# Three of VectorE's tiles move from the input projection to the output projection, half a gate changes its place, and two sums change engine

## The chip, the cores and the metric

The kernel runs on one core of a Trainium2 chip. The metric is the device time of one execution in microseconds; less is better. The core has a matrix engine (TensorE, in the profile PE), a vector engine (VectorE, DVE), an activation engine (ScalarE, ACT), GpSimd (POOL) and a queue engine (SyncE, SP) that issues nearly all transfers from memory.

## The reference, cut to what matters

One residual block over 256 tokens of width 2048, in float32:

```
mod = silu(c) @ w_ada + b_ada;  sh1, sc1, gt1, sh2, sc2, gt2 = split(mod, 6)
h   = rms_norm(x, g_mix) * (1 + sc1) + sh1
qA, kA, vA, qB, kB, vB = split(h @ w_in)
oA  = windowed attention (16 heads);  oB = chunked attention (16 heads)
x   = x + gt1 * (concat[rms_norm(oA), rms_norm(oB)] @ w_out)
h   = rms_norm(x, g_ffn) * (1 + sc2) + sh2
x   = x + gt2 * moe(h)         # 32 experts, w_gate, w_up, w_down: 403 MB
shf, scf = split(silu(c) @ w_ada_final + b_ada_final)
y   = rms_norm(x, g_final) * (1 + scf) + shf
```

The vectors of `mod` are matrix-vector products: one row `silu(c)` with a wide matrix. All weights are read once.

## The kernel before, in words

All weights go through a ring of six slots of 2 MB (`Ring`, lines 45 to 81). Tiles are loaded strictly in the order in which they were added to the ring, by SyncE (line 72 for a plain tile), and a tile can be sent for when the tile six places ahead of it, and all before that, have been released; on the chip the transfer waits until the slot's last reader is done.

After a first stage (the first quarters, qA, kA and vA), 20 steps follow. Twelve of them are halves of the rest of the input projection W_in (`in_step`: qB0, kB0, vB0, qB1, kB1, vB1, two steps each). Eight are the output projection W_out (`out_step`, called wo0 to wo7 here): wo0 to wo3 multiply the attention's A half with four column blocks of W_out, wo4 to wo7 its B half. Each step has one tile for TensorE. In the ring, `VECTOR_TILES` says how many tiles for VectorE follow it.

VectorE's tiles are the matrix-vector products: tiles of 512 rows by 1024 columns, four for a half of a vector. `vec_steps` works the queue of them off, four instructions a tile (line 382 for the first of a half, 384 for the others), each adding 128 rows into an accumulator of 128 x 1024. There are two accumulators. A half that has all four tiles is summed over the partitions by TensorE and copied out by ScalarE (`vec_finish`, three calls of `weave` later), and only then its accumulator is free. The halves of the first gate, gt1, keep theirs until `spread_gt1` has spread them over the partitions: at the start of wo1 for the first half, of wo3 for the second. `vec_steps` stops where it would need a third:

```
while queue and most and not (queue[0][1] == 0 and queue[0][4] == 0 and len(accs) == 2):
    vec_step(*queue.pop(0))
```

Attention heads are woven into the steps. `weave(n)` first runs what is due in `later`, then starts `n` heads from `ready`, makes the values of those two calls back and the transposes of those one call back, and runs the new heads' scores in four stages, with `vec_steps(2)` behind each stage. If no heads are left, there are no stages and no tile steps. `in_step` calls `weave(0)` and `weave(2)`, `out_step` `weave(1)` and `weave(2)`; between the two the step's tiles are put in the queue and `vec_steps(4)` is called, and after the step `vec_steps()` without a bound. The heads run out in wo2.

In `scores`, VectorE takes the masked maximum of a head (485, 486) and the reciprocal of its denominator (503), ScalarE the exponentials, and GpSimd scales (504, 505). `bias_B` sends for the bias of the pair of heads after next on ScalarE's queue, and GpSimd sets a corner of it (464). In `values`, the square of each pair's output (ScalarE, 538) is added to a running sum (539); when a kind's last head is through, `norm_o` makes the norm factors `rO[kind]` of it (546, then lines 190 to 198 on VectorE; `r_oB` in the profile). `out_step` evacuates every product with that factor and the gate (VectorE, 622; two banks, tag `w`) and adds it to x (623: GpSimd for A, VectorE for B).

After wo7 come four tiles for `shf`, the routing, and the expert layer: eight groups of four experts, gate, up and down, 403 MB through the same ring (829, 857).

Of the kernel before, what the change touches and what calls it, by code (L numbers as in the profile page):

```python
# [19 lines left out]
ALU = mybir.AluOpType  # L20
# [3 lines left out]
D = 2048  # L24
# [11 lines left out]
NEG = -1e30  # L36
RING = 6

VECTOR_TILES = [2, 3, 2, 3, 2, 3, 2, 3, 2, 3, 2, 3, 2, 2, 2, 2, 3, 2, 1, 0]


ROW_ADA, ROW_FIN, ROW_MIX, ROW_FFN, ROW_GFIN, ROW_OA, ROW_OB = 0, 24, 32, 36, 40, 44, 46
# [42 lines left out]
def block_kernel(ctx: ExitStack, tc: tile.TileContext, a: dict):  # L85
    nc = tc.nc
    V, S, G, PE = nc.vector, nc.scalar, nc.gpsimd, nc.tensor
# [8 lines left out]
    ada, fin = a["w_ada"], a["w_ada_final"]  # L96
    w_in, w_out = a["w_in"], a["w_out"]

    def rows(w, row, n, col, width):

        return w[row : row + 128 * n, col : col + width].rearrange("(k p) n -> p k n", p=128)
# [6 lines left out]
        first_quarters.append((gemv, [ring.add((2, 1536), rows(w_in, q * 512 + h * 256, 2, 0, 1536)) for h in range(2)]))  # L108

    vec_tiles = []  # L110
    for name, w, col in (("sh2", ada, 3 * D), ("sc2", ada, 4 * D), ("gt2", ada, 5 * D), ("gt1", ada, 2 * D), ("scf", fin, D), ("shf", fin, 0)):
        for c in (0,) if name == "shf" else (0, 1024):
            vec_tiles += [((name, c // 512), k, 4, 1024, rows(w, k * 512, 4, col + c, 1024)) for k in range(4)]
    blocks = [("qB0", 1536), ("kB0", 2560), ("vB0", 3584), ("qB1", 2048), ("kB1", 3072), ("vB1", 4096)]
    pe_tiles = [(name, h, rows(w_in, h * 1024, 8, col, 512)) for name, col in blocks for h in range(2)]
    pe_tiles += [("wo", h * 4 + n, rows(w_out, h * 1024, 8, n * 512, 512)) for h in range(2) for n in range(4)]
    order = []
    for (name, h, src), count in zip(pe_tiles, VECTOR_TILES):
        part = ring.add((8, 512), src)
# [9 lines left out]
    for g in range(8):  # L129
# [11 lines left out]
        else:  # L141
# [4 lines left out]
            for n in range(2):  # L146
                c = 1024 + 512 * n
# [63 lines left out]
    with ExitStack() as sa:  # L211
# [4 lines left out]
        def bank(tag, name, bufs=2):  # L216
            return ps.tile([128, 512], F32, tag=tag, name=name, bufs=bufs)
# [84 lines left out]
        for q, (gemv, parts) in enumerate(first_quarters):  # L302
# [3 lines left out]
            for i, idx in enumerate(gemv):  # L306
                w = ring.get(idx)
                for k in range(4):
                    c = cact[:, 4 * i + k : 4 * i + k + 1]
# [28 lines left out]
            for c in range(4):  # L338
                k = 4 * q + c
# [4 lines left out]
            for c in range(4):  # L344
                kk = 4 * q + c
                w = ring.get(parts[c // 2])[:, c % 2, :]
# [170 lines left out]
        def values(kind, h):  # L517
            pt = live.pop(("T", kind, h))
            c = h // 2
            b = 64 * (h % 2)  # L520
            if h % 2 == 0:
                live["o"] = bank("v", f"op{kind}{c}", 1)
            op = live["o"]
            if kind == "A":
                v, col = vA, (h // 4) * 64
            else:
                v, col = half[f"vB{h // 8}"], (h % 8) * 64
            PE.matmul(op[b : b + 64, 0:256], lhsT=v[:, 0, col : col + 64], rhs=pt[:, 0:256], start=True, stop=False, skip_group_check=True)
            PE.matmul(op[b : b + 64, 128:256], lhsT=v[:, 1, col : col + 64], rhs=pt[:, 256:384], start=False, stop=True, skip_group_check=True)
            if h % 2:  # L530
                cc = c + (8 if kind == "B" else 0)
                S.activation(oT[:, cc, :], op[:, 0:256], AF.Identity, scale=goutc[:, cc : cc + 1])
                s = sq[kind]
                if c == 0:
                    S.activation(s, op[:, 0:256], AF.Square)
                else:
                    s2 = pa2.tile([128, SEQ], F32, tag="sq", name=f"sq{kind}{c}", bufs=1)
                    S.activation(s2, op[:, 0:256], AF.Square)
                    G.tensor_tensor(s, s, s2, op=ALU.add)
                if h == 15:  # L540
                    later.append([1, lambda: norm_o(kind)])

        def norm_o(kind):
            pm = bank("m", f"pn{kind}", 1)
            for t in range(2):
                PE.matmul(pm[:, t : t + 1], lhsT=sq[kind][:, t * 128 : (t + 1) * 128], rhs=ones[:, 0:1], start=True, stop=True)
            rO[kind] = rsqrt_mean(pm[:, 0:2], 1.0 / 1024, 2, f"o{kind}")
# [3 lines left out]
        def weave(n=1):  # L551

            for item in list(later):
                item[0] -= 1
                if item[0] <= 0:
                    later.remove(item)
                    item[1]()
            if not n:
                return
            batch, ready[:] = ready[:n], ready[n:]  # L560
            line.insert(0, batch)
            for depth, step in ((2, values), (1, turn)):
                if len(line) > depth:
                    for item in line[depth]:
                        step(*item)
            heads = [scores(*item) for item in batch]
            while heads:
                heads = [x for x in heads if next(x, "end") is None]
                vec_steps(2)
            del line[3:]  # L570
# [400 lines left out]
    for g in range(8):  # L971
# [56 lines left out]
        else:  # L1028
# [3 lines left out]
            for fc in range(4):  # L1032
                w = ring.get(dn[fc])
# [6 lines left out]
            for fc in range(2):  # L1040
                w = ring.get(dn[4 + fc])
# [4 lines left out]
            for n in range(2):  # L1046
                w = ring.get(dn[6 + n])
# [20 lines left out]
    for J, y in last.items():  # L1068
        c = slice(J * 512, (J + 1) * 512)
# [3 lines left out]
    for t, J, store in ((0, 0, 0), (0, 1, 2), (0, 2, 0), (0, 3, 2), (1, 0, 1)):  # L1073
        c = slice(J * 512, (J + 1) * 512)
        V.scalar_tensor_tensor(big[:, t, c], big[:, t, c], r3[:, t : t + 1], shbc[:, c], op0=ALU.mult, op1=ALU.add)
        if store:
            c = slice((J + 1 - store) * 512, (J + 1) * 512)
# [27 lines left out]
```

## Time and profile before

| | |
|---|---|
| median of 3 runs | 1508.41 us (1505.83 to 1509.24) |
| the profiled execution | 1502.64 us, its span 1501.0 us |
| TensorE (PE) | 1188.0 us busy, 79% of the span |
| VectorE (DVE) | 499.0 us, 33% |
| ScalarE (ACT) | 166.2 us, 11% |
| GpSimd (POOL) | 157.5 us, 10% |
| transfers | 599.38 MB, 399 GB/s on the mean |
| mean granted clock of TensorE | 0.917 |

The shares are averages over the span. The input projection with its attention heads lies between some 150 and 358 us, the output projection from there to 520 us, the routing around 530 us and the expert layer after 543 us. Times in the profile are microseconds from the span's start. A matmul of float32 stands as two instructions. A granted clock of 1.00 is TensorE's full clock. A DMA share of about 1.03 is what the busiest stretches show.

### The profile page before, as it was taken

What the parts mean: (1) busy time and instruction counts of PE and PEld (TensorE: products, weight loads), DVE (VectorE), ACT (ScalarE), POOL (GpSimd) and SP (SyncE); (2) the same over time, 40 slices, a digit from 0 to 9 for tenths busy, and PEclk for the clock granted to TensorE, in tenths of its full rate; (3) what the DMA queues carried; (4) which work ended last, traced back from release to release, by engine and by line L of the source; (5) the groups of instructions that cost most, each with busy time, mean ns of one, the idle gap of its engine ahead of it and who ended that gap; (6) DMA issues with size and microseconds to landing.
All of it is one profiled execution on the core that took longest, in us unless ns stands there. A gap on an engine that the chain in (4) does not pass through costs nothing.

```text
span 1501.0 us, 14175 instructions
## 1 busy us (share of the span) xinstructions
PE 1188.0 (79%) x5891; PEld 525.8 (35%) x5892; DVE 499.0 (33%) x807; ACT 166.2 (11%) x423; POOL 157.5 (10%) x144
## 2 busy tenths in 40 slices
PE   4889999999999997777677767766767667667786
PEld 2667865754444542222212212211211211221222
DVE  1453789887667531011111211111201201111113
ACT  2000222223220110000000100000000000000012
POOL 1000355523441100000000000000000000000002
PEclk9999999999999999978978889889889988997999
DMA  9999999999987999999999999999999999999995
GB/s 333 396 392 399 394 402 402 402 401 400 355 317 302 388 380 422 421 420 421 421 421 421 421 421 422 422 422 421 421 420 422 422 422 422 421 421 421 421 412 210
DMA packets 125470, 599.38 MB, mean 399 GB/s; under 512 B 5881, under 2 KB 8489, under 8 KB 78041
## 3 DMA queue, kind: packets, MB, share of 16 engines
q1 hardware_dynamic: 121248, 594.82, 98.1%
q10 hardware_dynamic: 4120, 3.57, 0.7%
q8 instruction: 48, 0.79, 0.2%
q14 instruction: 22, 0.17, 0.0%
q0 software_dynamic: 32, 0.02, 0.0%
HBM read 596.02 MB, written 2.12 MB: 398 GB/s over the span
## 4 chain that ended last, share of the span: by engine, by line
DMA 45%; PE 11%; SPq 0%; issue 0%; ACT 0%; DVE 0%; ACTq 0%; DVEq 0%
DMA ring<-w_down 23%; DMA ring<-w_up 12%; DMA ring<-w_gate 10%; PE yp L857 5%; PE gp L829 2%; PE up L829 2%; PE sc_g L876 0%; SPq L70 0%; PE bc L770 0%; PE bc L771 0%; PE last L1060 0%; PE last L1059 0%; ACT big L1071 0%; PE last L1070 0%; ACTq L1072 0%
## 5 line engine op out<-in xcount | busy, mean ns | idle before, releaser
L857 PE MATMUL yp<-ring,actT_g 128*32 128x512 f32 x1024 | 181.5, 763 | 97.5 <-DMA ring<-w_down 91.7
L829 PE MATMUL up<-ring,xg_g 128*32 128x512 f32 x1024 | 177.3, 721 | 73.3 <-DMA ring<-w_up 73.2
L829 PE MATMUL gp<-ring,xg_g 128*32 128x512 f32 x1024 | 169.9, 703 | 69.3 <-DMA ring<-w_gate 68.8
L878 DVE TENSOR_TENSOR x<-x,sc_g 128x512 f32<-128x512 f32 x64 | 44.0, 688 | 252.3 <-PE sc_g L876 252.3
L618 PE MATMUL po<-ring,oT 128*128 128x512 f32 x256 | 118.0, 617 | 1.4 <-DMA ring<-w_out 1.4
L857 PEld LDWEIGHTS yp<-ring,actT_g 128*32 128x32 f32 x1024 | 39.3, 133 | 225.6 <-DMA ring<-w_down 130.9
L881 POOL TENSOR_TENSOR big<-x,xg_gscf 128x512 f32<-128x512 f32 x8 | 10.0, 1272 | 958.8 <-DVE x L878 958.8
L799 DVE TENSOR_SCALAR xg_g<-g_g,gsc,sh2c 128x128 f32<-128x128 f32 x64 | 26.2, 410 | 249.8 <-PE g_g L790 232.5
L829 PEld LDWEIGHTS up<-ring,xg_g 128*32 128x32 f32 x1024 | 38.4, 127 | 197.5 <-DMA ring<-w_up 105.9
L829 PEld LDWEIGHTS gp<-ring,xg_g 128*32 128x32 f32 x1024 | 38.0, 123 | 186.5 <-DMA ring<-w_gate 99.5
L797 ACT ACTIVATE xg_g<-g_g,sh2c,gsc 128x128 f32<-128x128 f32 x64 | 29.3, 458 | 503.9 <-DVE xg_g L799 503.9
L384 DVE SCALAR_TENSOR_TENSOR acc_gt<-ring,cact,acc_gt 128x1024 f32<-128x1024 f32 x60 | 79.2, 1321 | 1.6
L870 DVE TENSOR_TENSOR ys_g<-yp,gt2bc 128x512 f32<-128x512 f32 x32 | 21.8, 690 | 171.8 <-PE yp L857 171.8
L618 PEld LDWEIGHTS po<-ring,oT 128*128 128x128 f32 x256 | 49.7, 198 | 63.6 <-issue 61.1
L790 PEld LDWEIGHTS g_g<-pn_g,big 128*128 128x128 f32 x512 | 60.5, 194 | 29.1 <-issue 28.2
L790 PE MATMUL g_g<-pn_g,big 128*128 128x128 f32 x512 | 66.7, 284 | 1.4 <-DVE pn_g L782 1.4
L348 PE MATMUL qA<-hT,ring 128*128 128x256 f32 x256 | 61.6, 396 | 4.8 <-DVE hT L343 3.5
L876 PE MATMUL sc_g<-ys_g,smat_g 128*128 128x512 f32 x128 | 63.4, 618 | 1.6 <-DVE ys_g L870 1.6
L585 PE MATMUL pw_vB<-ring,hT 128*128 128x512 f32 x128 | 56.7, 597 | 2.9 <-DMA ring<-w_in 2.9
L589 PE MATMUL pw_kB<-hT,ring 128*128 128x256 f32 x256 | 57.0, 381 | 1.2 <-DMA ring<-w_in 1.2
L589 PE MATMUL pw_qB<-hT,ring 128*128 128x256 f32 x256 | 56.5, 381 | 0.2 <-DMA ring<-w_in 0.2
L348 PEld LDWEIGHTS qA<-hT,ring 128*128 128x128 f32 x256 | 50.7, 199 | 13.1 <-DVE hT L343 4.3
(329 smaller groups left out, 1125.4 us busy)
## 6 DMA issues: line engine op xcount, KB each, us to landing
ring<-w_gate SPq DMA_DIRECT2D x64, 2048.0 KB, 20.3
ring<-w_up SPq DMA_DIRECT2D x64, 2048.0 KB
ring<-w_down SPq DMA_DIRECT2D x62, 2048.0 KB, 20.4
ring<-w_ada SPq DMA_DIRECT2D x32, 2048.0 KB, 17.0
ring<-w_ada SPq DMA_DIRECT2D x32, 1024.0 KB, 14.1
ring<-w_ada_final SPq DMA_DIRECT2D x16, 2048.0 KB, 11.0
ring<-w_in SPq DMA_DIRECT2D x12, 2048.0 KB, 16.8
ring<-w_out SPq DMA_DIRECT2D x8, 2048.0 KB
```

The lines of the kernel that those rows point to most:

```text
L348: PE.matmul(early[n // 2][:, (n % 2) * 256 : (n % 2 + 1) * 256], lhsT=w[:, n * 128 : (n + 1) * 128], rhs=hT[:, kk, :], start=kk == 0 and n ...
L384: V.scalar_tensor_tensor(accs[name], w[:, kk, :], cact[:, c : c + 1], accs[name], op0=ALU.mult, op1=ALU.add)
L585: PE.matmul(b[s], lhsT=hT[:, kk, s * 128 : (s + 1) * 128], rhs=w[:, k, :], start=kk == 0, stop=kk == 15)
L589: PE.matmul(b[s][:, n * 256 : (n + 1) * 256], lhsT=w[:, k, c * 128 : (c + 1) * 128], rhs=hT[:, kk, :], start=kk == 0 and n == 0, stop=kk = ...
L618: PE.matmul(b, lhsT=oT[:, (i // 4) * 8 + k, t * 128 : (t + 1) * 128], rhs=w[:, k, :], start=k == 0, stop=k == 7)
L790: PE.matmul(pm[:, i * 128 : (i + 1) * 128], lhsT=big[:, t, kk * 128 : (kk + 1) * 128], rhs=pn[:, t, :], start=t == 0 and i == 0, stop=t == ...
L797: S.activation(xg[:, kk, :], pm[:, i * 128 : (i + 1) * 128], AF.Identity, bias=sh2c[:, kk : kk + 1], scale=gsc2[:, kk : kk + 1])
L799: V.tensor_scalar(xg[:, kk, :], pm[:, i * 128 : (i + 1) * 128], gsc2[:, kk : kk + 1], sh2c[:, kk : kk + 1], op0=ALU.mult, op1=ALU.add)
L829: PE.matmul(bankt[32 * e : 32 * e + 32, :], lhsT=xg[:, kk, 32 * e : 32 * e + 32], rhs=w[e // 2][:, e % 2, j, :], start=kk == 0, stop=kk == ...
L857: PE.matmul(y[32 * e : 32 * e + 32, :], lhsT=aT[:, fc, 32 * e : 32 * e + 32], rhs=w(e)[:, n * 512 : (n + 1) * 512], start=fc == 0, stop=fc ...
L876: PE.matmul(pm, lhsT=sm[:, t * 128 : (t + 1) * 128], rhs=ys[:, n, :], start=True, stop=True)
L878: V.tensor_tensor(x1[:, t, c], x1[:, t, c], pm, op=ALU.add)
```

## The change

Three of the tiles that VectorE works on move from the steps of W_in (30 before, 27 now) to those of W_out (14 before, 17 now). Four tiles of the second gate, its second half, move behind the first gate, so that the order of the halves becomes sh2, sh2, sc2, sc2, gt2, gt1, gt1, gt2, scf, scf, shf. In `values`, the last addition of each kind's squares is made by VectorE and not by GpSimd.

```diff
-VECTOR_TILES = [2, 3, 2, 3, 2, 3, 2, 3, 2, 3, 2, 3, 2, 2, 2, 2, 3, 2, 1, 0]
+VECTOR_TILES = [2, 2, 3, 2, 2, 2, 3, 2, 2, 3, 2, 2, 3, 2, 3, 3, 3, 2, 1, 0]
...
     vec_tiles = []
-    for name, w, col in (("sh2", ada, 3 * D), ("sc2", ada, 4 * D), ("gt2", ada, 5 * D), ("gt1", ada, 2 * D), ("scf", fin, D), ("shf", fin, 0)):
-        for c in (0,) if name == "shf" else (0, 1024):
-            vec_tiles += [((name, c // 512), k, 4, 1024, rows(w, k * 512, 4, col + c, 1024)) for k in range(4)]
+    halves = [(n, w, col, c) for n, w, col in (("sh2", ada, 3 * D), ("sc2", ada, 4 * D), ("gt2", ada, 5 * D), ("gt1", ada, 2 * D), ("scf", fin, D), ("shf", fin, 0)) for c in (0, 1024)]
+    for i in (0, 1, 2, 3, 4, 6, 7, 5, 8, 9, 10):
+        name, w, col, c = halves[i]
+        vec_tiles += [((name, c // 512), k, 4, 1024, rows(w, k * 512, 4, col + c, 1024)) for k in range(4)]
...
                     S.activation(s2, op[:, 0:256], AF.Square)
-                    G.tensor_tensor(s, s, s2, op=ALU.add)
+                    (V if h == 15 else G).tensor_tensor(s, s, s2, op=ALU.add)
                 if h == 15:
```

In the texts below, the first half of a vector is called a, its second half b, and a tile of it has a number from 0: gt2b[0] is the first tile of gt2's second half.

## Rows read from the trace of the kernel before

**Rows 1.** Chain of waits that ended last: start us, us, what.
```profile
675.54 24.84 DMA ring<-w_up
...
1425.80 24.72 DMA ring<-w_down
```

**Rows 2.** Windows: engines' busy us (instructions), granted clock, DMA share, GB/s.
```profile
320.00:340.00 20.00, 17.15 (x64) 8.38 (x66) 16.92 (x30) 5.10 (x16) 3.89 (x6) 1.00 1.04 400
380.00:400.00 20.00, 17.86 (x50) 8.24 (x50) 10.59 (x26) 5.38 (x18) 8.31 (x8) 0.84 1.03 401
420.00:440.00 20.00, 20.00 (x62) 9.17 (x62) 14.77 (x23) 4.09 (x15) 10.03 (x9) 1.00 0.72 270
460.00:480.00 20.00, 20.00 (x53) 9.32 (x52) 17.06 (x15) 1.45 (x4) 4.21 (x2) 1.00 0.58 215
```

**Rows 3.** TensorE's waits, 150 to 362 us: us in total, times, longest.
```profile
PE pw_vB L585 <- DMA ring<-w_in: 2.9, 1, 2.9
PE po L618 <- DMA ring<-w_out: 1.4, 1, 1.4
PE pw_kB L589 <- DMA ring<-w_in: 1.2, 1, 1.2
PE pw_qB L589 <- DMA ring<-w_in: 0.2, 1, 0.2
```

**Rows 4.** TensorE's timeline: start us, us, instruction, idle before and releaser.
```profile
381.20 1.13 PE L427 MATMUL pm_bc<-acc_gt,ones 128*128 128x512 f32 x2
...
383.02 7.03 PE L618 MATMUL po<-ring,oT 128*128 128x512 f32 x16
...
396.27 9.18 PE L618 MATMUL po<-ring,oT 128*128 128x512 f32 x16
...
439.62 7.03 PE L618 MATMUL po<-ring,oT 128*128 128x512 f32 x16
...
451.54 0.95 PE L546 MATMUL pnB<-ones,sqB 128*128 128x1 f32 x4 [3.12 <-POOL sqB L539]
```

**Rows 5.** TensorE's groups, 358 to 540 us: busy, mean ns, idle before.
```profile
L512 PE MATMUL tpB<-ident,stB 128*128 128x128 f32 x30 | 6.2, 305 | 2.7 <-POOL stB L505 1.7 <-POOL stB L504 0.8
L528 PE MATMUL opB<-ptB,vB 128*64 128x256 f32 x16 | 4.5, 405 | 0.8 <-ACT sqB L538 0.8
```

**Rows 6.** VectorE's timeline, the same columns as in rows 4.
```profile
359.77 5.24 DVE L384 SCALAR_TENSOR_TENSOR acc_gt<-ring,cact,acc_gt 128x1024 f32<-128x1024 f32 x4
...
398.74 0.73 DVE L382 TENSOR_SCALAR acc_scf<-ring,cact 128x1024 f32<-128x1024 f32 x1
399.50 3.92 DVE L384 SCALAR_TENSOR_TENSOR acc_scf<-ring,cact,acc_scf 128x1024 f32<-128x1024 f32 x3
...
447.42 6.46 DVE L384 SCALAR_TENSOR_TENSOR acc_scf<-ring,cact,acc_scf 128x1024 f32<-128x1024 f32 x4
453.81 0.15 DVE L190 TENSOR_SCALAR rv_oB<-pnB 128x2 f32<-128x2 f32 x1
...
455.02 0.16 DVE L198 TENSOR_TENSOR r_oB<-r_oB,rl_oB 128x2 f32<-128x2 f32 x1
462.59 0.75 DVE L622 SCALAR_TENSOR_TENSOR hT<-po,r_oB,hT 128x512 f32<-128x512 f32 x1 [7.41 <-PE po L618]
...
463.99 5.97 DVE L384 SCALAR_TENSOR_TENSOR acc_scf<-ring,cact,acc_scf 128x1024 f32<-128x1024 f32 x4
...
481.78 0.74 DVE L622 SCALAR_TENSOR_TENSOR hT<-po,r_oB,hT 128x512 f32<-128x512 f32 x1
```

**Rows 7.** GpSimd: one group (min, median, max ns), two rows of its timeline.
```profile
L505 POOL TENSOR_SCALAR stB<-stB,denB x16: 917/920/1989, 314.0 to 436.2; 128x256 f32<-128x256 f32 x16
...
404.73 0.20 POOL L464 MEMSET biasB<- 64x128 f32 x1 [9.48 <-DMA biasB<-scratch]
...
449.79 1.70 POOL L539 TENSOR_TENSOR sqB<-sqB,sqB 128x256 f32<-128x256 f32 x1
```

**Rows 8.** The ring's transfers, 420 to 470 us, from issue to landing.
```profile
DMA to landing us min/median/max: 11.7/11.7/11.7
```

## Prediction

> **What bounds the kernel now.** I read the chain of waits first. From 675 us on it alternates between a weight transfer of some 25 us and a short product [rows 1]: the expert layer runs at the rate of the transfers, so it only moves as a whole. Whatever changes the time happens before it. Second, the windows of 20 us: the DMA share, 1.03 where the engines are full, falls to 0.72 and 0.58 in two stretches of the output projection [rows 2], which lose (0.31 + 0.45) x 20 / 1.03 = 15 us of transfer. That looks like an offer, but TensorE is busy 20.00 of 20 us in both: transfers stop because slots of the ring come free late, and they come free at the pace of TensorE and VectorE. So the question is whether the change makes *TensorE* reach the expert layer sooner. Third, TensorE's waits in the input projection: four, 5.7 us together, all for tiles of the ring [rows 3]. Fourth, TensorE's timeline of the output projection [rows 4] and the groups of its small waits [rows 5]. Fifth, VectorE's timeline between the steps wo3 and wo5, because the second half of that projection can't be evacuated without `r_oB`, which VectorE makes [rows 6].
>
> **The order that the change gives.** VectorE is in order, and `vec_steps` stops when a tile would open a third accumulator. I worked the new lists through `vec_steps`, `weave` and `later` by hand; the same working on the old lists gives the order of [rows 6] (a tile inside wo3, one at its end, then `rv_oB`).
>
> - wo0 brings gt1b[3] and gt2b[0], [1]. gt1a and gt1b hold both accumulators, so the two gt2b tiles stand still until `spread_gt1(1)` opens wo1.
> - wo1 then runs four tiles instead of two. gt2b ends in its second weave; its finish is due three weaves later, in wo3.
> - wo2 brings scfa[0..2], but gt1b (until wo3) and gt2b hold both accumulators: VectorE runs no tile at all in wo2.
> - wo3 has no heads left, and `weave` runs tiles only between the stages of heads. scfa[0] goes in `vec_steps(4)`; the other five (scfa[1..3], scfb[0], [1]) go in the last `vec_steps()`, in one piece. Behind them in VectorE's queue stands `norm_o` of B, which makes `r_oB`. Before, one tile stood there.
>
> **The sum.** *Gain in the input projection.* Three tiles leave it, 2.1 MB each at 401 GB/s [rows 2], 5.2 us each, 16 us of transfer. TensorE can get back only what it waited: 5.7 us [rows 3]. Bounds: 0 and 16 us. I take 5.7, since apart from these waits its matmuls stand back to back. wo1 then starts at 381.2 - 5.7 = 375.5 [rows 4].
>
> *wo1 to wo3.* Before, wo1 lost 2.5 us (0.6 of it in wo0) to GpSimd's scaling and 0.8 to ScalarE [rows 5], and one product took 9.18 us where 7.03 is usual [rows 4]. Earlier arrival should save half of the first (1.3), the 0.8 and the 2.1 of the slow product: 4.2 us. New there: head 11's scaling. Its VectorE steps now have tile steps between them: the first evacuation comes at 384.3 (wo1's first product ends 383.02 + 7.03 - 381.20 = 8.8 us in [rows 4]), two steps follow, and the masked maxima end behind TensorE's scores at some 390.6. The bias that is sent for then takes some 8 us to land (GpSimd stood 9.48 us for one [rows 7]), to 398.3. GpSimd then scales; the larger of its two operations takes 0.92 us at best and 1.99 at worst [rows 7]. TensorE wants the result at 397.8 (its second product ends at 396.8, and values come first) and waits 2.1 to 4.4 us; I take 3.5, nearer the worst, because six tile steps run beside it. Heads 12 and 13: VectorE has from 384.3 on sixteen steps at 5.24 / 4 (21 us), two evacuations (1.5) and some 4.8 us of three heads' maxima, reciprocals and waiting, so their reciprocal comes at 411.6; four scalings later, at 414.7, TensorE can turn them, wants to at 413.1, and loses 2.1 us with the transpose that it can't overlap (bounds 0 and 4). gt2b's finish moves ahead of the point that I compare at: 1.0. Together 3.5 + 2.1 + 1.0 - 4.2 = 2.4 us lost. Call T3 the end of wo3's second product: before 439.62 + 7.03 = 446.65 [rows 4], after 446.65 - 5.7 + 2.4 = 443.3. **Lead 3.3 us**, bounds -0.9 (both new waits followed by a slow product, 2.1 each) and 10.2 (neither new wait, and all the old ones gone).
>
> *The five tiles.* From T3: evacuation and the moved sum end at T3 + 2.1: the evacuation takes 0.75, the sum then waits for ScalarE's square until some T3 + 1.7, and takes 0.4, half of the evacuation of twice the elements [rows 6]. Then one tile at 5.9 beside GpSimd's last sum (463.99 row; 6.46 at worst), three at 5.24 and one that opens an accumulator, 0.73 + 3.92, which with its gap is 4.7 [rows 6]: 26.3 us. Then `rv_oB` to `r_oB`, 1.4 us (453.81 to 455.18). `r_oB` is there at T3 + 29.8. Before, wo4's first evacuation began at 462.59 = T3 + 15.9, and from it to wo5's first took 19.2 us of VectorE alone (to 481.78 [rows 6]). That stays, for the same tiles stand between. TensorE has two banks for these products: it fills both in wo4 and stands until `r_oB` empties one. It has no slack to make this up: 20.00 of 20 us busy from 460 on [rows 2].
>
> So lag = 29.8 - 15.9 - lead = 13.9 - 3.3 = **10.6 us**.
>
> *What costs nothing.* wo4's tile waits for a slot freed at T3 + 8 at the latest and lands 11.7 us later [rows 8], wo5's at T3 + 23.1 + 11.7: both products are done before VectorE asks (T3 + 49 for wo5). The moved sums: for B, GpSimd's 1.70 us at 449.79 [rows 7] held TensorE for 3.1 us [rows 4], and VectorE would give 2.8 of that back; but what follows is `r_oB`, now behind five tiles, so it buys nothing. If these were out of the way it would be worth its 2.8. For A, VectorE waits for a square once in the input projection, at most two tile steps, 2.6 us; its tile work there has shrunk by 16 us, so I cost it at nothing. The gate ahead of half of the second: gt1 is ready earlier than it is asked for, and gt2 is only asked for in the expert layer.
>
> *Through to the end.* The ring holds six tiles and the first expert tiles wait in it for TensorE, so the lag reaches the transfers whole. The profiled execution's 1502.64 us become 1513.2. It lies 5.8 below the median of the three runs shown, 1508.41; on that median the forecast is **1519.0 us**.
>
> **A rule that speaks against it.** The 9.18 us product stands right behind short idle stretches [rows 4], in a window whose granted clock is 0.84 on average; the input projection's 2.9 us wait [rows 3] lies in one of 1.00 [rows 2]. So a wait may bring the lower of the two levels (1.2 GHz of 2.4) or not, and I count none of the new waits so. The Trainium skill ("TensorE: Matmul & The Clock Gate", section "HAM oscillation — how this bites in real kernels") says that idle stretches put TensorE back to its lower clock, and that this is paid at each of them. By it the waits in wo1 and wo2 would each slow a product, the lead would be -0.9 and the sum 14.8; the idle time in wo4 would slow one too, under VectorE's work.
>
> **Rivals.**
> 1. *Forecast, +5 to +13: chance 0.62.* The five tiles gate `r_oB`.
> 2. *TensorE slow after each new wait: 0.14.* For it: the 9.18 us product. Against: the 2.9 us wait with a clock of 1.00. Two products at 2.1 more: lag 14.8, time 1523.2; with a third behind wo4's wait that VectorE doesn't cover, 1525.3.
> 3. *Faster: 0.12.* scfa finds an accumulator in wo2, so that wo3 ends with one tile as before. It decides at one point: whether gt2b's finish comes before scfa's first step is offered in wo2. Against: the count of three weaves, which I read from the code alone. Then the sum of B's squares pays its 2.8, the lead 3.3, and 1508.41 - 6.1 gives 1502.3.
> 4. *The change doesn't reach the end (same): 0.12.* The block is there but the lead is near its bound of 10.2 or beyond, because the input projection was paced by transfers more than its waits tell (bound 16). At 10.2 the lag is 3.7, 1512.1; from 10.9 on it is lost in the measurement, at 13.9 it is gone. Against: TensorE's 20.00 of 20.
>
> **Numbers.** A measurement of this kernel tells about 0.2% (3 us) from no change. Slower: 1 and 2, 0.76. Same 0.12, faster 0.12. The likeliest case alone is 1513 to 1522. The range goes up past rival 2's 1525.3 and down to 1507, inside rival 4, which leaves out rival 3 and a part of 4: 1507 to 1526.
>
> **What would show it.** In the profile after: no wait for w_in in the input projection, and wo1 starting near 375; in wo2 no tile step on VectorE; behind wo3's last evacuation twenty tile steps in one piece and `rv_oB` only after them, near T3 + 28; TensorE waiting in wo5 for VectorE's evacuation of wo4, and a DMA share well under 1 around it; the first expert product some 10 us later than before. The prediction is wrong if tile steps stand in wo2, if `r_oB` comes within 20 us of T3, or if TensorE reaches T3 before 436.

## The result, and the profile after

| | before | after |
|---|---|---|
| median | 1508.83 us (1505.83 to 1509.60, 4 runs) | 1520.49 us (1518.36 to 1521.76, 4 runs) |
| the profiled execution | 1502.64 us | 1519.70 us |

The change makes the kernel slower: the ratio is 1.0080, with a 95% interval of 1.0061 to 1.0098. The forecast was 1519.0 us.

TensorE's waits of the change between 150 and 352 us (in total, times, longest) come first. Of the 5.7 us of [rows 3], 4.3 for w_in and 1.4 for wo0's tile of w_out, nothing is left; 2.0 us of other waits stand there instead:

```profile
PE pm_rr L445 <- ACT R_shf L407: 0.7, 1, 0.7
PE pnA L547 <- ACT R_gt L407: 0.7, 1, 0.7
PE tpA L513 <- POOL stA L506: 0.6, 1, 0.6
```

Then TensorE's timeline of the change, from wo0 to wo5; it answers to [rows 4]:

```profile
357.12 7.03 PE L619 MATMUL po<-ring,oT 128*128 128x512 f32 x16
...
369.66 8.43 PE L619 MATMUL po<-ring,oT 128*128 128x512 f32 x16
...
380.17 1.12 PE L428 MATMUL pm_bc<-acc_gt,ones 128*128 128x512 f32 x2
...
395.12 9.35 PE L619 MATMUL po<-ring,oT 128*128 128x512 f32 x16
...
442.12 7.03 PE L619 MATMUL po<-ring,oT 128*128 128x512 f32 x16
...
451.77 0.58 PE L547 MATMUL pnB<-ones,sqB 128*128 128x1 f32 x4 [1.83 <-DVE sqB L540]
460.38 16.01 PE L619 MATMUL po<-ring,oT 128*128 128x512 f32 x32 [8.03 <-DMA ring<-w_out]
...
482.51 10.01 PE L619 MATMUL po<-ring,oT 128*128 128x512 f32 x16 [4.08 <-DMA ring<-w_out]
```

wo1 starts at 380.17, 1.0 us earlier than before, and T3 is 442.12 + 7.03 = 449.15, 2.5 us *later* than before. Two slow products (8.43 and 9.35 us) stand on the way where before had one. After T3 TensorE waits twice for tiles of W_out, 8.0 and 4.1 us. In wo0 GpSimd, which scales for TensorE's transposes, stood at the corner of a bias tile until 364.86:

```profile
364.86 0.20 POOL L465 MEMSET biasB<- 64x128 f32 x1 [10.15 <-DMA biasB<-scratch]
```

VectorE's timeline of the change, which answers to [rows 6]:

```profile
440.83 0.74 DVE L383 TENSOR_SCALAR acc_scf<-ring,cact 128x1024 f32<-128x1024 f32 x1
...
450.76 0.87 DVE L540 TENSOR_TENSOR sqB<-sqB,sqB 128x256 f32<-128x256 f32 x1 [0.75 <-ACT sqB L539]
451.55 15.80 DVE L385 SCALAR_TENSOR_TENSOR acc_scf<-ring,cact,acc_scf 128x1024 f32<-128x1024 f32 x12
467.27 0.74 DVE L383 TENSOR_SCALAR acc_scf<-ring,cact 128x1024 f32<-128x1024 f32 x1
468.05 9.21 DVE L385 SCALAR_TENSOR_TENSOR acc_scf<-ring,cact,acc_scf 128x1024 f32<-128x1024 f32 x7
477.18 0.15 DVE L191 TENSOR_SCALAR rv_oB<-pnB 128x2 f32<-128x2 f32 x1
...
478.40 0.16 DVE L199 TENSOR_TENSOR r_oB<-r_oB,rl_oB 128x2 f32<-128x2 f32 x1
478.69 0.75 DVE L623 SCALAR_TENSOR_TENSOR hT<-po,r_oB,hT 128x512 f32<-128x512 f32 x1
...
497.85 0.74 DVE L623 SCALAR_TENSOR_TENSOR hT<-po,r_oB,hT 128x512 f32<-128x512 f32 x1
```

The twenty steps stand there in one piece, 12 + 1 + 7, from 451.55 to 477.2, where [rows 6] have four (447.42). `r_oB` is there at 478.56, wo4's first evacuation at 478.69, 16.1 us later than before, and wo5's at 497.85, again 16.1 later. The windows of the change (columns as in rows 2) show where VectorE stood before that:

```profile
420.00:440.00 20.00, 19.43 (x60) 8.77 (x61) 2.71 (x13) 4.32 (x14) 7.59 (x9) 1.00 0.65 245
440.00:460.00 20.00, 10.52 (x36) 4.79 (x35) 15.94 (x14) 3.09 (x5) 2.97 (x2) 0.86 0.64 235
```

From 420 to 440 us VectorE is busy 2.71 of 20 us where before had 14.77 [rows 2], while scfa's tiles lie in the ring; from 451.55 on it works without a pause, and TensorE waits for slots of the ring that VectorE's tiles hold (between 400 and 465 us SyncE stands 28.9 us behind VectorE's steps before it can send for a tile). The first expert product starts at 559.09 us, 15.8 later than before: the lag goes through to the end.

### The profile page after: what moved, and what is told of

It reads as the page before. It is cut to its first block, busy times and chain, and to the rows that moved or that the text cites. A ratio compares the mean times of both kernels' runs of the same rounds, so it can differ in the third digit from the quotient of the medians.

```text
span 1518.0 us, 14175 instructions
## 1 busy us (share of the span) xinstructions
PE 1194.9 (79%) x5891; PEld 528.4 (35%) x5892; DVE 496.9 (33%) x809; ACT 166.7 (11%) x423; POOL 149.2 (10%) x142
## 4 chain that ended last, share of the span: by engine, by line
DMA 51%; PE 19%; DVE 2%; SPq 0%; issue 0%; ACT 0%; POOL 0%; ACTq 0%
DMA ring<-w_down 26%; DMA ring<-w_gate 13%; DMA ring<-w_up 12%; PE yp L858 5%; PE po L619 4%; PE gp L830 3%; PE up L830 3%; DVE acc_scf L385 1%; PE shift L692 1%; DMA ring<-w_out 1%; PE lg L660 0%; PE bc L771 0%; PE bc L772 0%; SPq L70 0%; PE x1t L644 0%; PE g_g L791 0%
## 5 line engine op out<-in xcount | busy, mean ns | idle before, releaser
L830 PE MATMUL gp<-ring,xg_g 128*32 128x512 f32 x1024 | 175.4, 722 | 71.4 <-DMA ring<-w_gate 70.9
L830 PE MATMUL up<-ring,xg_g 128*32 128x512 f32 x1024 | 171.8, 698 | 69.2 <-DMA ring<-w_up 69.2
L619 PE MATMUL po<-ring,oT 128*128 128x512 f32 x256 | 121.5, 631 | 12.1 <-DMA ring<-w_out 12.1
L349 PEld LDWEIGHTS qA<-hT,ring 128*128 128x128 f32 x256 | 51.6, 203 | 13.7 <-DVE hT L344 4.3
```

Of the source, the lines that this page charges most:

```text
L349: PE.matmul(early[n // 2][:, (n % 2) * 256 : (n % 2 + 1) * 256], lhsT=w[:, n * 128 : (n + 1) * 128], rhs=hT[:, kk, :], start=kk == 0 and n ...
L619: PE.matmul(b, lhsT=oT[:, (i // 4) * 8 + k, t * 128 : (t + 1) * 128], rhs=w[:, k, :], start=k == 0, stop=k == 7)
L830: PE.matmul(bankt[32 * e : 32 * e + 32, :], lhsT=xg[:, kk, 32 * e : 32 * e + 32], rhs=w[e // 2][:, e % 2, j, :], start=kk == 0, stop=kk == ...
```

## The experiments

Every ratio is to the kernel before, run beside it on the same chip, with its 95% interval behind it. In the code, `V` is VectorE and `G` GpSimd.

**Does the order of the gates alone do it? (order_only)** The kernel before with the new order of the halves; the numbers of tiles and the sums stay as they were.

```diff
+    for i in (0, 1, 2, 3, 4, 6, 7, 5, 8, 9, 10):
+        name, w, col, c = halves[i]
```

> The kernel before with the new order of the gates alone; the numbers of tiles stay, GpSimd makes the sums. Theory (it is the accumulators that gt1 holds through wo0 to wo2 that pile five tiles up at wo3's end): twenty steps in one piece there as in the change, time 1518 to 1526, no better than the change although not one tile moved. Rival (the three moved tiles are what costs): 1506 to 1512, as before.

Measured: 1.0086 (1.0058 to 1.0113), 1520.39 us. VectorE's timeline of that run:

```profile
452.32 17.03 DVE L385 SCALAR_TENSOR_TENSOR acc_scf<-ring,cact,acc_scf 128x1024 f32<-128x1024 f32 x12
469.27 0.75 DVE L383 TENSOR_SCALAR acc_scf<-ring,cact 128x1024 f32<-128x1024 f32 x1
470.05 9.21 DVE L385 SCALAR_TENSOR_TENSOR acc_scf<-ring,cact,acc_scf 128x1024 f32<-128x1024 f32 x7
479.18 0.15 DVE L191 TENSOR_SCALAR rv_oB<-pnB 128x2 f32<-128x2 f32 x1
```

The same twenty steps, and the same loss, without one moved tile. The half gate that is put behind gt1 makes the pile.

**Is it the accumulators? (own_acc)** The whole change, but gt2b adds up in the space of kA and vA, which nothing reads any more by wo0, and `vec_steps` doesn't count it.

```diff
-                accs[name] = pa2.tile([128, 1024], F32, tag="acc", ...)[:, 0 : 4096 // n]
+                accs[name] = bflat[:, 0:1024] if name == ("gt2", 2) else pa2.tile([128, 1024], F32, tag="acc", ...)[:, 0 : 4096 // n]
...
-            while queue and most and not (... and len(accs) == 2):
+            while queue and most and not (... and queue[0][0] != ("gt2", 2) and len(accs.keys() - {("gt2", 2)}) == 2):
```

> The change whole, but gt2's second half has an accumulator of its own, in the space of kA and vA, which the output projection no longer reads, and isn't counted by `vec_steps`. Theory (accumulators): no tile stands still; scfa runs in wo2, two tiles stand between wo3 and `r_oB` instead of five, `r_oB` near T3 + 14 instead of T3 + 29.5, the loss is gone: 1503 to 1509. Rival (VectorE and the ring can't carry 17 tiles in the output projection in any order): 1514 or more.

Measured: 0.9985 (0.9970 to 0.9999), 1503.56 us. VectorE's timeline of that run, the two tiles that are left in front of `r_oB`, and it:

```profile
451.16 0.74 DVE L383 TENSOR_SCALAR acc_scf<-ring,cact 128x1024 f32<-128x1024 f32 x1
451.94 9.21 DVE L385 SCALAR_TENSOR_TENSOR acc_scf<-ring,cact,acc_scf 128x1024 f32<-128x1024 f32 x7
...
462.28 0.16 DVE L199 TENSOR_TENSOR r_oB<-r_oB,rl_oB 128x2 f32<-128x2 f32 x1
```

T3 is 448.76 there (a product at 441.73 of 7.03 us), so `r_oB` comes at T3 + 13.7 instead of T3 + 29.4, with the same 17 tiles in the output projection. With this order, the held accumulators are the loss.

**Is it the place of `r_oB`, or VectorE's work? (norm_early)** The change with four of the five tiles taken out from in front of `norm_o`: two behind it, ahead of wo4's products, the rest in wo4.

```diff
+                vec_steps(8)        # in out_step, i == 4, behind the loop that runs norm_o
...
-            vec_steps()
+            vec_steps(4 if name == "wo" and h == 3 else 99)
```

> The change with only one tile ahead of `norm_o` at wo3's end, two more between `norm_o` and wo4's products, and the rest of the pile in wo4. Theory A (VectorE's work is the bound from wo3's end on: eight tiles stand between T3 and wo5's first evacuation whichever comes first): `r_oB` comes near T3 + 9, yet wo5's first evacuation stays within 6 us of the change's T3 + 48.7, time 1514 to 1521. Theory B (only the place of `r_oB` in the queue costs, as the prediction's chain has it): wo5's first evacuation back near T3 + 35 and the time 1507 to 1511.

Measured: 1.0091 (1.0064 to 1.0118), 1521.26 us: as the change. VectorE's and then TensorE's timeline of that run:

```profile
460.33 0.16 DVE L199 TENSOR_TENSOR r_oB<-r_oB,rl_oB 128x2 f32<-128x2 f32 x1
460.41 10.52 DVE L385 SCALAR_TENSOR_TENSOR acc_scf<-ring,cact,acc_scf 128x1024 f32<-128x1024 f32 x8
472.17 0.75 DVE L624 SCALAR_TENSOR_TENSOR hT<-po,r_oB,hT 128x512 f32<-128x512 f32 x1 [1.24 <-PE po L620]
...
480.43 16.52 DVE L385 SCALAR_TENSOR_TENSOR acc_scf<-ring,cact,acc_scf 128x1024 f32<-128x1024 f32 x12
496.88 0.74 DVE L624 SCALAR_TENSOR_TENSOR hT<-po,r_oB,hT 128x512 f32<-128x512 f32 x1
```

```profile
462.91 16.02 PE L620 MATMUL po<-ring,oT 128*128 128x512 f32 x32 [8.15 <-DMA ring<-w_out]
487.10 8.99 PE L620 MATMUL po<-ring,oT 128*128 128x512 f32 x16 [8.17 <-DMA ring<-w_out]
```

T3 is 451.55 here. `r_oB` comes at T3 + 8.9, twenty microseconds sooner, and wo5's first evacuation at T3 + 45.3 instead of T3 + 48.7. Up to there VectorE waits 1.24 us for TensorE and otherwise works almost without a pause; the pile stands behind `r_oB` now, holds the ring's slots (TensorE waits 8.17 us for wo5's tile) and ends nearly as late. The time lies 0.3 us above theory A's range and 10 above theory B's. So theory A: what costs is the work that was put off, and its place in the queue hardly matters. wo5's first product ends at 496.09, 0.8 us before VectorE takes it; so this run doesn't tell VectorE's time from the ring's slots that its tiles hold meanwhile.

**What is the sum of the squares worth? (sums_only, after_gsum)** The last edit alone on the kernel before, and the change without it.

```diff
-                    G.tensor_tensor(s, s, s2, op=ALU.add)
+                    (V if h == 15 else G).tensor_tensor(s, s, s2, op=ALU.add)
```

> The kernel before with the two last sums on VectorE and nothing else. Theory (the sum of B's squares stands between wo3 and `norm_o`, and one tile behind it is short enough not to hide it): the 3.1 us wait of TensorE in front of pnB falls to about 1 us, `r_oB` comes 0 to 2 us earlier, the time falls by 2 to 3 us, to about 1506. Rival (VectorE's tile, 6.5 us, gates `r_oB` anyway, and the ring hides the rest): within 1 us of before.

> The change without its last edit: GpSimd makes the two last sums again. Theory (behind five tiles the sum gates nothing): as the change, ratio to before 1.006 to 1.011, `r_oB` within 1 us of the change's T3 + 29.4. Rival (the sum helps here as much as it did alone, 0.43%): 1.012 or more.

Measured: alone 0.9957 (0.9940 to 0.9975), 6.5 us faster by the ratio (3.8 to 9.0), more than the 2 to 3 us of the theory; the change without it 1.0089 (1.0061 to 1.0116), not told apart from the change with it (1.0080; such a pair shows a difference from some 0.3% on). TensorE's timeline of sums_only; then the window of 440 to 460 us, first of sums_only, then of the kernel before:

```profile
451.43 0.58 PE L546 MATMUL pnB<-ones,sqB 128*128 128x1 f32 x4 [0.86 <-DVE sqB L539]
451.87 20.85 PE L618 MATMUL po<-ring,oT 128*128 128x512 f32 x48
```

```profile
440.00:460.00 20.00, 19.14 (x56) 8.49 (x55) 14.61 (x19) 3.29 (x6) 2.97 (x2) 1.00 0.98 374
440.00:460.00 20.00, 16.89 (x39) 7.35 (x38) 12.72 (x15) 3.17 (x6) 5.08 (x3) 0.83 0.98 372
```

pnB comes 2.6 us after T3 (448.79: a product at 441.76 of 7.03 us), before 4.9 [rows 4]: 2.3 us. And the three products behind it take 20.85 us; in the kernel before they took 23.88, and the granted clock of the window was 0.83. Behind the wait of 3.1 us stood another 3.0 in slow products. These 5.3 us are what the traces show of the 6.5; what the sum of A's squares adds isn't separated. Inside the change nothing of it counts: in after_gsum pnB starts at 456.71, VectorE comes to it only at 479.45, behind the same twenty steps, and `r_oB` is there at T3 + 29.0.

**Are the moved tiles worth anything without the pile? (tiles_only, old_order_333, late_memset)** The old order of the gates with moved tiles; in the second and third with VectorE's sums and `VECTOR_TILES` ending in 3, 3, 3, 2, 3, 2, 1, 0; in the third `bias_B` no longer sets the corner of the bias tile, but `scores` does when the pair's first head comes.

```diff
-            G.memset(bt[0:64, :, 0:64], NEG)          # bias_B
...
+                if h % 2 == 0:                         # scores, kind B
+                    G.memset(bias_tiles[h // 2][0:64, :, 0:64], NEG)
```

> The kernel before with the new numbers of tiles alone: three tiles move, the order of the gates and the sums stay. No tile stands still then; two tiles instead of one stand between wo3 and `r_oB`. Theory (the moved tiles are neither the loss nor a gain: what the input projection gives back is waited for again in wo0): within 0.3% of before. Rival (the moved tiles alone fill VectorE): 0.5% slower or more.

> Three tiles moved to wo0, wo1 and wo2 (3, 3, 3, 2, 3, 2, 1, 0), the old order of the gates, the last sums on VectorE: one tile stands between wo3 and `r_oB`, as before. Theory (the relief of the input projection is given back in wo0, to GpSimd, which stands behind the memset that waits for the next bias): as the sums alone, ratio 0.993 to 0.997. Rival (the removed waits reach the end): 0.992 or less.

> As the run with 3, 3, 3, 2, 3, 2, 1, 0, but the corner of a bias tile is set when its first head comes and not when it is sent for, so that GpSimd's scaling doesn't stand behind a transfer. Theory (that memset's wait for the bias is what takes the relief back in wo0, and what TensorE waits for in wo1): TensorE's waits for GpSimd between 352 and 412 us fall from some 4 us to under 1, the slow products behind them go, 3 to 8 us faster than the run without it. Rival (the scaling itself is too slow next to VectorE's tiles): within 2 us of it.

Measured: 1.0052 (1.0032 to 1.0072), 1.0031 (1.0017 to 1.0044) and 1.0039 (1.0024 to 1.0054). None of the three theories held, for one reason that I had not seen (that tiles_only and late_memset lie near their rivals' numbers says nothing for these, for the same reason). With three tiles fewer in front of wo0, the old order brings gt1a[3] only *with* wo0, behind `spread_gt1(0)`. So these three kernels leave the last tile out of the sum that gates the first 512 columns, and their output is not the block's. And at the spreads of wo0 and wo2 TensorE stands until VectorE has caught up. TensorE's timeline of old_order_333:

```profile
359.81 2.04 PE L427 MATMUL pm_bc<-acc_gt,ones 128*128 128x512 f32 x2 [4.42 <-DVE denB L503]
...
417.08 2.08 PE L427 MATMUL pm_bc<-acc_gt,ones 128*128 128x512 f32 x2 [4.47 <-DVE acc_gt L384]
```

Two waits of 4.4 and 4.5 us; behind both the spread itself is slow (2.04 and 2.08 us for 1.12), and behind the first a product too (8.31). The moved tiles need the first gate ahead; the first gate ahead makes the pile. These runs say nothing of the tiles by themselves.

**The tiles without pile and without that wait (own_acc_333, own_333_late, sums_late).** own_acc with the ending 3, 3, 3, 2, 3, 2, 1, 0, which leaves one tile in front of `r_oB`; the same with the corner set late; and sums_only with the corner set late, in which no tile moves.

> The change with gt2b's own accumulator, and the three moved tiles beside wo0, wo1 and wo2 (3, 3, 3, 2, 3, 2, 1, 0) so that one tile, not two, stands between wo3 and `r_oB`. Theory (what own_acc still lacks to the sums alone is the second tile in front of `r_oB`): `r_oB` near T3 + 9, wo4's first evacuation set by TensorE again, ratio to before 0.993 to 0.997, as the sums alone. Rival (the third tile in wo1 costs GpSimd and TensorE what it saves in wo4): 0.998 or more, as own_acc.

> The run before with the corner of a bias tile set when its first head comes. Theory (part of TensorE's waits for GpSimd in wo0 is a memset that waits for a transfer): TensorE's waits for GpSimd between 352 and 412 us fall by 1 to 3 us, and the time by as much; rival (GpSimd's scaling itself is late): within 1 us of the run before.

> The kernel before with the last sums on VectorE and the corner of a bias tile set when its first head comes; no tile moves. Theory: TensorE's 3.9 us of waits for GpSimd in wo0 and wo1 fall to under 2 and the slow product of wo1 goes: ratio to before 0.991 to 0.994, better than the sums alone (0.9957). Rival (the wait moves to the scaling or to the transfer of the tile): as the sums alone.

Measured: 0.9971 (0.9955 to 0.9987), 0.9947 (0.9928 to 0.9966) and 0.9918 (0.9893 to 0.9943); medians 1500.48, 1497.30 and 1492.73 us. The first stands at the edge of its theory's range, with `r_oB` at T3 + 8.9 as expected; the second gains 3.2 us on it, with TensorE's waits for GpSimd between 352 and 412 us down from 5.5 us to 3.0; the third lies in its range. It is the fastest version of this study, ahead of both kernels. TensorE's starts of wo1 and wo2 in own_333_late, then in sums_late:

```profile
374.75 1.12 PE L428 MATMUL pm_bc<-acc_gt,ones 128*128 128x512 f32 x2
...
403.19 1.12 PE L428 MATMUL pm_bc<-acc_gt,ones 128*128 128x512 f32 x2
```

```profile
383.51 1.12 PE L427 MATMUL pm_bc<-acc_gt,ones 128*128 128x512 f32 x2
...
405.64 1.12 PE L427 MATMUL pm_bc<-acc_gt,ones 128*128 128x512 f32 x2
```

With the tiles moved, wo1 starts 8.8 us earlier, and takes 28.4 us instead of 22.1. By T3 (445.60 against 443.06) the lead is gone and 2.5 us more. TensorE's waits for GpSimd between 352 and 412 us, own_333_late first; the 3.0 us there lie all in wo1, the 1.1 of sums_late in wo0:

```profile
PE tpB L514 <- POOL stB L507: 1.7, 2, 1.3
PE tpB L514 <- POOL stB L506: 1.3, 1, 1.3
```

```profile
PE tpB L513 <- POOL stB L506: 1.1, 2, 0.6
```

So the late corner does what was meant where few tiles stand beside the heads: TensorE's waits for GpSimd fall from 3.9 us in sums_only to 1.1, and wo1's second product takes 7.13 us instead of 8.99 (one in wo0 takes 8.40 instead of 7.13). With three tiles in wo1 GpSimd is late without any transfer, because VectorE is. The reciprocal that the scaling needs stands behind four tile steps there, behind two in sums_late, and the scaling itself is slower beside the steps that follow. VectorE's last steps before the reciprocal and GpSimd's first scaling in own_333_late, then that scaling in sums_late:

```profile
378.64 5.24 DVE L385 SCALAR_TENSOR_TENSOR big<-ring,cact,big 128x1024 f32<-128x1024 f32 x4
384.13 1.54 POOL L506 TENSOR_SCALAR stB<-stB,denB 128x128 f32<-128x128 f32 x1 [6.28 <-DVE denB L505]
```

```profile
389.98 0.60 POOL L505 TENSOR_SCALAR stB<-stB,denB 128x128 f32<-128x128 f32 x1 [3.63 <-DVE denB L504]
```

TensorE is through with wo1's values at 384.4 in own_333_late, and gets its transpose at 385.73; in sums_late the scaling is done before TensorE comes. Of wo1's 6.3 us more, 3.1 are such waits, and the rest is slower instructions behind them (granted clock 0.84 and 0.82 from 380 to 400 us, 1.00 in sums_late). After 412 us another 2.9 us of waits for GpSimd follow, none in sums_late.

## Why the prediction was right, and where it wasn't

- *The order.* Right, row by row: no tile step in wo2, one tile inside wo3, five at its end. order_only and own_acc show that it is the two held accumulators.
- *The five tiles.* Forecast 26.3 us and `r_oB` at T3 + 29.8; measured 25.7 (451.55 to 477.2) and T3 + 29.4. (The moved sum took 0.87 us, not 0.4.) wo5's first evacuation was forecast for T3 + 49 and came at T3 + 48.7.
- *The lead at T3.* The term that was mis-sized: 3.3 us forecast, -2.5 measured. The step that failed is the gain in the input projection, taken as 5.7 us in full at wo1's start, with wo0 put at no loss. wo0's first product did start 4.3 us earlier (357.12 against 361.44), but wo0 gave 3.3 of it back, and 1.0 was left. TensorE came to its transposes before GpSimd had scaled, because GpSimd stood at the corner of a bias tile until its transfer had landed. That came only 2.7 us earlier than before (364.86 against 367.54). TensorE's waits for GpSimd between 352 and 412 us rose from 2.5 us to 4.5, and a second product, in wo0, ran slow. I had let the earlier arrival *save* waits. The steps' lengths from wo1 on are 28.1, 22.9 and 18.0 us; the forecast comes to 27.3 (before's 28.0 with 3.5 and -4.2), 22.5 and 18.0. In wo1 that is luck: neither the 4.2 was saved (ScalarE's wait and a slow product are there still) nor did the new 3.5 come (the waits for GpSimd are 2.1 us, before 2.0). A part of the lead can be the executions' own difference: norm_early, the same code up to T3, reaches it 2.4 us later than the change (451.55), and there is one trace of each.
- *The sum.* So the lag was 16 us in the profiles, not 10.6, near rival 2's 14.8. The medians differ by 11.7 only, because the profiled execution of before lies 6 us below its median and that of after 0.8. The forecast of the median, 1519.0, is 1.5 us off; a good part of that is luck, since the mis-sized lead and this difference went against each other.
- *Rival 2 and the clock.* Half right. Slow products followed the waits in wo0 and wo1 (8.43 and 9.35 us, the granted clock 0.66 from 390 to 400 us), none followed the 1.6 us of waits in wo2, whose next product took 7.13. In after_gsum 1.1 us of waits at the same place were followed by one of 9.71. So the length of the waits alone doesn't tell; what does, these runs don't show. The Trainium skill's section cited above ("TensorE: Matmul & The Clock Gate") tells of waits for transfers between groups of matmuls. It bears on these short waits by likeness only: the first two products fit it, the change's wo2 doesn't.
- *What gates wo4.* I had `r_oB`'s place in the queue as the chain. norm_early shows that the work behind it would have come nearly as late wherever `r_oB` stands; the sum comes out the same, by another chain than mine.
- *The sums' price.* "It buys nothing" inside the change: after_gsum's trace bears it out, its time within the noise. "2.8 if it were out of the way" was too little: 6.5 alone (3.8 to 9.0), as the slow products behind the wait go too.
- *The gate's order.* I costed it at nothing by itself and saw the pile as the sum of two edits. It is the edit that makes the loss, and the moved tiles can't be had without it, which I didn't say.
- *Rival 3 and 4.* scfa found no accumulator in wo2, and the lag did reach the end, whole.
- *Signs that didn't come.* wo1 starts at 380.17, not near 375. In wo5 TensorE waits for the tile (482.51), not for the evacuation, which ended at 479.4. And the DMA share is 1.02 around it, from 460 to 500 us; the low ones (0.65 from 420 to 440 us, 0.64 from 440 to 460) lie earlier, in and behind the stretch in which VectorE's tiles stand still in the ring.

## What to carry to other kernels

A queue that stops for want of a buffer doesn't lose only the stop: the work comes back later as a pile, and the pile lands on whatever stands next. Before you change the order in which halves of accumulators open, write down for each step which are held, by whom and until when. A wait taken from a busy engine is worth its time only if what it meets next is ready as well; look at the next two engines in the chain before you book it.

## What the hardware showed that I had not expected

A short wait of TensorE can cost twice: 3.1 us of waiting in front of pnB were followed by 3.0 us of slow products, and with 2.3 us of the wait these went too. But the input projection's 2.9 us wait of before lies in a window with a clock of 1.00.

GpSimd's scaling of 128 x 128 and 128 x 256 takes 0.60 and 0.92 us with no accumulating tile step beside it, and 1.03 and 1.67 with one, as GpSimd's and VectorE's timelines of the change show in wo1:

```profile
388.70 0.60 POOL L505 TENSOR_SCALAR stB<-stB,denB 128x128 f32<-128x128 f32 x1
389.29 0.92 POOL L506 TENSOR_SCALAR stB<-stB,denB 128x256 f32<-128x256 f32 x1
390.19 1.03 POOL L505 TENSOR_SCALAR stB<-stB,denB 128x128 f32<-128x128 f32 x1
391.20 1.67 POOL L506 TENSOR_SCALAR stB<-stB,denB 128x256 f32<-128x256 f32 x1
```

```profile
389.79 0.96 DVE L383 TENSOR_SCALAR acc_gt<-ring,cact 128x1024 f32<-128x1024 f32 x1
390.79 1.28 DVE L385 SCALAR_TENSOR_TENSOR acc_gt<-ring,cact,acc_gt 128x1024 f32<-128x1024 f32 x1
```

The step at 389.79 opens an accumulator and reads one tile; the scaling beside it still takes 0.92 us. The step at 390.79 reads the tile and the accumulator, and the two scalings that share 0.43 and 0.87 us with it are 0.43 and 0.75 longer. The Trainium skill ("SBUF — State Buffer", section "Who interferes with whom") says that a VectorE instruction with two inputs in SBUF contends with a GpSimd instruction that reads SBUF; these rows agree. This, and the reciprocal behind the tile steps, is how tiles moved beside the attention heads cost TensorE time through GpSimd, an engine that is busy 10% of the span.
